# A two-layer hybrid diffusion trunk on one core: the channel mixer written as seven block products, in two phases, with the output feature-major

## The chip, the cores and the metric

One core of a Trainium2 chip runs the whole program. The metric is device time in microseconds (us) of one execution. The kernel before took 2927.19 us (median of three runs, 2924.78 to 2929.57).

Five engines share the work: PE (TensorE) does the matmuls, DVE (VectorE), ACT (ScalarE) and POOL (GpSimd) do elementwise work, and SP issues the DMAs. PE accumulates in eight PSUM banks (the tile PS, 8 x 512 columns); everything else lies in SBUF or in DRAM.

## What is computed

1,024 sample tokens and 128 prompt tokens, T = 1152 columns in all, pass two layers of width 1024. Layer 0 mixes tokens by latent attention and retention, layer 1 by a chunked gated MLP (gMLP). Each layer ends with the part that the change rewrites, the SwiGLU channel mixer with d_ff = 2816 = 22 tiles of 128:

```python
def swiglu(h, w_gate, w_up, w_down):
    return (jax.nn.silu(h @ w_gate) * (h @ w_up)) @ w_down
...
        hp = modulate(rmsnorm(xp, norm_g[l, 1]), sh2p, sc2p)
        hs = modulate(rmsnorm(xs, norm_g[l, 1]), sh2s, sc2s)
        xp = xp + g2p * swiglu(hp, w_ffn_gate[l], w_ffn_up[l], w_ffn_down[l])
        xs = xs + g2s * swiglu(hs, w_ffn_gate[l], w_ffn_up[l], w_ffn_down[l])
    y_prompt = rmsnorm(xp, final_norm_g)
    y_sample = rmsnorm(xs, final_norm_g)
```

Prompt and sample columns have their own shift, scale and gate (from `c_ctx` and `c`, the "conditioning"), so a piece of columns that crosses column 1024 is evicted in two instructions.

## The kernel before

Activations lie feature-major: the residual x is four tiles XT of [128, 2, 1152], read as eight feature tiles `X(f)`. Every large product is done in float32 precision by splitting both operands into a high part (ACT cast to fp32r) and a low part (DVE or POOL subtraction), and taking three passes: high x high, high x low, low x high (`groupA`, `three`). The split normalised activations are Hh and Hl in the tiles hq.

Columns go in three chunks of 384 (`CHUNKS`). In the channel mixer (`ffn`), a gate/up unit j takes two weight tiles and does, for each chunk, 8 x 3 matmuls for gate and 8 x 3 for up; ACT takes the silu out of PSUM, DVE multiplies, ACT and DVE split the result into one of three HID tiles in SBUF. After two units a down step `dn(j)` takes two rows of the down weight and does for each chunk and each of eight output tiles m 2 x 3 matmuls, and `resid` adds the bank onto x on DVE (`SCALAR_TENSOR_TENSOR x<-PS,mod,x`). So gate/up and down alternate, and the inner activations never leave SBUF.

Weights come through `Stream`: three staging slots ST of 512 KB, filled by SP, are split (`prep`) into a ring of five tiles RING (w). Background work (norms, squares, final output) stands in the queues `bg` and `bg2`; `fill` and `tick` issue it between products where the estimate of `Clocks` says that it won't hold up PE. PSUM banks rotate (`nxt`), so an eviction has several products' time.

`xnorm` normalises one chunk of 384 for the next block; the sum of squares over features is a matmul by ones. At the end `y_trans` turns x back by PE transposes (identity matmuls of 128 columns), `y_out` scales and SP stores token-major rows to o_ys and o_yp.

All instructions are recorded by one helper, so every row of the trace reads L126 (after the change L129); go by tiles and shapes.

Of the kernel before, what the change touches and what calls it, by code (L numbers as in the profile page):

```python
# [13 lines left out]
P = 128  # L14
# [3 lines left out]
CHUNKS = [(0, 384), (384, 384), (768, 384)]  # L18
NF = 22
# [20 lines left out]
class Clocks:  # L40
    """An estimate of when each engine is free and each piece of memory ready, to choose what to issue next."""
# [73 lines left out]
class Timed:  # L115
    """An engine whose instructions are also entered in the clocks."""
# [13 lines left out]
def body(nc, tc, ap):  # L130
# [45 lines left out]
    rgd = dp.tile([4, P, T], F32, name="rgd")  # L176

# [9 lines left out]
    sm = sb.tile([P, 5, 8], F32, name="sm")  # L187
    make_identity(nc, ident)
# [9 lines left out]
    att = [False]  # L198

    def nxt():  # L200
        if att[0]:
            return PS[:, 7]
        b = bank_i[0]
        bank_i[0] = step_bank(b)
        return PS[:, b]
# [9 lines left out]
    class Stream:  # L215
# [11 lines left out]
        def pump(self, force=False):  # L227
            moved = True
            while moved:
# [18 lines left out]
                if self.pi < self.di and self.pi not in self.stops:  # L248
                    it = self.items[self.pi]
                    now = clk.t["T"] + 1.0  # L250
                    if it["kind"] == "w":
# [37 lines left out]

        def take(self):  # L290
# [34 lines left out]
    def fill(aps=()):  # L325
        """Issues background work that does not hold up the tensor engine's next product, which reads aps."""
# [29 lines left out]
    def ada_raw(l, b, k, half):  # L356
        def fn(v):
            if k == 0 and half == 0 and ada_f:
                drain(ada_f.pop())
            for j in (2 * half, 2 * half + 1):  # L360
                o = (j % 2) * 512
                mm(ada_bank[32 * j:32 * j + 32], S32[:, k], v[:, o:o + 512], k == 0, k == 7)
            if k == 7 and half == 1:
                ada_f.append(ada_fin(l, b))
                bg.appendleft(ada_f[-1])
        src = ap["w_ada"][l, k * P:(k + 1) * P, 2048 * b + 1024 * half:2048 * b + 1024 * half + 1024]
        W.add(src, [1024], "raw", fn)
# [60 lines left out]
    def squares(ci, srcs, first=True, eng=V):  # L428
        acc = nt(ci % 2)
        for i, s in enumerate(srcs):  # L430
            n = s.shape[-1]
            if first and i == 0:
                S.activation(acc[:, :n], s, AF.Square)
            else:
                sqi[0] ^= 1
                q = nt(5 + sqi[0], n)
                S.activation(q, s, AF.Square)
                eng.tensor_tensor(acc[:, :n], acc[:, :n], q, ALU.add)
            yield

# [19 lines left out]
    def norm(ci, srcs, dh, dl, cnt, c0, n, A, B, f32out=None):  # L460
        yield [nt(ci % 2, n)]
        scale_cols(ci, cnt, n)
        yield [nt(2, n)]
        scale_bc(n)
        yield
        r = nt(2, n)
        m = len(srcs)
        ts = [nt(3 + i % 4, n) for i in range(m)]
        sg = [(cond, slice(s0 - c0, s0 - c0 + ln)) for cond, s0, ln in segs(c0, n)]

        def first(i):
            if i % 4 == 3:
                G.tensor_tensor(ts[i], srcs[i], r, ALU.mult)
                return
            for cond, s in sg:
                V.scalar_tensor_tensor(ts[i][:, s], srcs[i][:, s], A(i, cond), r[:, s], ALU.mult, ALU.mult)

        def high(i):
            if i % 4 == 3:
                for cond, s in sg:  # L480
                    S.activation(ts[i][:, s], ts[i][:, s], AF.Identity, scale=A(i, cond), bias=B(i, cond))
            if B is None or i % 4 == 3:
                S.copy(R(dh[i]), ts[i])
# [1488 lines left out]
```

## Time and profile before

| | us |
|---|---|
| median of three runs | 2927.19 |
| lowest, highest | 2924.78, 2929.57 |
| span of the profiled execution, first to last instruction | 2919.6 |
| median less that span | 7.6 |
| PE busy | 2846.6 (97%) |
| DVE, ACT, POOL busy | 1309.1 (45%), 849.6 (29%), 311.9 (11%) |
| mean granted TensorE clock | 0.989 |

The page gives no other time for the profiled execution than its span, so sums are made against the span, and the 7.6 us are added at the end. The channel mixers are the stretches from about 860 to 1740 us (layer 0) and from about 2090 to 2910 us (layer 1). Matmuls overlap in the pipeline of PE, so the mean ns of one is longer than the distance from one start to the next; the price of a matmul in a dense run is that distance.

### The profile page before, as it was taken

What the parts mean: (1) busy time and instruction counts of PE and PEld (TensorE: products, weight loads), DVE (VectorE), ACT (ScalarE), POOL (GpSimd) and SP (SyncE); (2) the same over time, 40 slices, a digit from 0 to 9 for tenths busy, and PEclk for the clock granted to TensorE, in tenths of its full rate; (3) what the DMA queues carried; (4) which work ended last, traced back from release to release, by engine and by line L of the source; (5) the groups of instructions that cost most, each with busy time, mean ns of one, the idle gap of its engine ahead of it and who ended that gap; (6) DMA issues with size and microseconds to landing.
All of it is one profiled execution on the core that took longest, in us unless ns stands there. A gap on an engine that the chain in (4) does not pass through costs nothing. (4 is left out here: it accounts for less than half of the span.)

```text
span 2919.6 us, 40063 instructions
## 1 busy us (share of the span) xinstructions
PE 2846.6 (97%) x16583; PEld 2698.9 (92%) x16583; DVE 1309.1 (45%) x2478; ACT 849.6 (29%) x1575; POOL 311.9 (11%) x235
## 2 busy tenths in 40 slices
PE   6999998999999999999999999999999999999999
PEld 5986897888989899999999987999999999999999
DVE  5651235888463333333443354354533334333433
ACT  5552224776251111111111143232411111111115
POOL 1120013665110000000000031000100000000001
PEclk8999998999999999999999999999999999999999
DMA  8395426322322212222211131141111111111111
GB/s 293 88 276 173 136 78 187 83 78 79 116 73 87 77 61 87 87 75 85 66 37 36 44 109 36 33 127 30 45 43 44 44 44 43 36 38 44 44 30 65
DMA packets 223467, 237.62 MB, mean 81 GB/s; under 512 B 15595, under 2 KB 193526, under 8 KB 221750
## 3 DMA queue, kind: packets, MB, share of 16 engines
q1 hardware_dynamic: 220880, 232.23, 26.3%
q8 instruction: 130, 2.13, 0.3%
q10 hardware_dynamic: 2406, 2.85, 0.3%
q14 instruction: 51, 0.42, 0.0%
HBM read 193.37 MB, written 41.66 MB: 81 GB/s over the span
## 5 line engine op out<-in xcount | busy, mean ns | idle before, releaser
L126 PE MATMUL PS<-hq,w 128*128 128x384 f32 x9216 | 1650.7, 338 | 12.3 <-ACT hq L126 7.4
L126 PEld LDWEIGHTS PS<-hq,w 128*128 128x128 f32 x9216 | 1615.1, 188 | 48.3 <-ACT SC L126 14.7
L126 PE MATMUL PS<-h,w 128*128 128x384 f32 (+1 forms) x3182 | 563.4, 337 | 3.5 <-DVE x L126 3.5
L126 PEld LDWEIGHTS PS<-h,w 128*128 128x128 f32 (+1 forms) x3182 | 554.2, 188 | 11.3 <-DVE x L126 10.0
L126 DVE SCALAR_TENSOR_TENSOR x<-PS,mod,x 128x384 f32<-128x384 f32 (+2 forms) x768 | 371.3, 513 | 228.1 <-PE PS L126 227.6
L126 DVE TENSOR_TENSOR w<-ST,w 128x1024 fp32r<-128x1024 f32 (+1 forms) x201 | 232.2, 1165 | 496.8 <-ACT w L126 496.5
L126 ACT ACTIVATE SC<-PS 128x384 f32<-128x384 f32 (+1 forms) x162 | 80.3, 496 | 895.4 <-PE PS L126 889.4
L126 DVE TENSOR_TENSOR SC<-PS,SC 128x384 f32<-128x384 f32 (+2 forms) x139 | 77.5, 558 | 458.3 <-PE PS L126 454.7
L126 ACT CAST w<-ST 128x1024 fp32r<-128x1024 f32 (+1 forms) x201 | 194.6, 980 | 102.4 <-PE PS L126 80.0
L126 ACT CAST h<-SC 128x384 fp32r<-128x384 f32 (+2 forms) x141 | 72.1, 511 | 495.4 <-DVE SC L126 493.3
L126 POOL TENSOR_TENSOR SC<-SC 128x384 f32<-128x384 f32 x35 | 35.6, 1017 | 1602.8 <-ACT SC L126 1600.5
L126 PE MATMUL PS<-w,hq 128*128 128x512 f32 x648 | 158.6, 402 | 1.4 <-POOL hq L126 1.3
L126 PEld LDWEIGHTS PS<-w,hq 128*128 128x128 f32 x648 | 122.0, 191 | 39.7 <-issue 10.3
L126 DVE TENSOR_TENSOR h<-SC,h 128x384 fp32r<-128x384 f32 (+2 forms) x141 | 79.4, 563 | 83.7 <-ACT h L126 83.5
L126 PE MATMUL PS<-w,w 96*128 96x512 f32 x384 | 108.5, 418 | 3.9 <-ACT w L126 2.4
L126 DVE TENSOR_REDUCE sm<-PS 128x1 f32<-128x1152 f32 (+1 forms) x72 | 89.0, 1236 | 22.1 <-PE PS L126 21.3
L126 DVE TENSOR_TENSOR x<-PS,x 128x512 fp32r<-128x512 f32 (+2 forms) x161 | 94.5, 623 | 0.8
L126 PEld LDWEIGHTS PS<-w,w 96*128 96x128 f32 x384 | 69.1, 194 | 17.0 <-issue 3.0
L126 PE MATMUL PS<-x,hq 128*128 128x256 f32 x504 | 77.4, 296 | 5.1 <-DVE sm L126 5.1
L126 ACT CAST x<-PS 128x512 fp32r<-128x512 f32 (+2 forms) x161 | 79.4, 546 | 6.4 <-PE PS L126 4.9
L126 PEld LDWEIGHTS PS<-x,hq 128*128 128x128 f32 x504 | 68.4, 194 | 9.5 <-DVE sm L126 6.2
L126 POOL TENSOR_TENSOR SC<-x,SC 128x384 f32<-128x384 f32 x24 | 28.8, 1200 | 446.1 <-ACT SC L126 395.8
(163 smaller groups left out, 1831.7 us busy)
## 6 DMA issues: line engine op xcount, KB each, us to landing
ST<-in_w_ada SPq DMA_DIRECT2D x80, 512.0 KB, 3.9
ST<-in_w_ffn_gate SPq DMA_DIRECT2D x44, 512.0 KB, 3.9
ST<-in_w_ffn_up SPq DMA_DIRECT2D x44, 512.0 KB, 4.9
ST<-in_w_ffn_down SPq DMA_DIRECT2D x44, 512.0 KB, 3.6
ST<-in_w_in_ab SPq DMA_DIRECT2D x19, 512.0 KB, 4.9
xtd<-x SPq DMA_DIRECT2D x24, 384.0 KB, 6.3
x<-xtd SPq DMA_DIRECT2D x24, 384.0 KB, 4.5
hq<-in_w_ada SPq DMA_DIRECT2D x8, 1024.0 KB, 11.8
```

Of the source, the lines that this page charges most:

```text
L126: return fn(*args, **kw)
```

## The change

**Column pieces.** The chunks of the two output projections and of gMLP's u become four pieces of 288 (`NAT`, or `PAIRED`: 0, 2, 1, 3). x is laid out anew as `xh(c, q)`: c is the first or second 288 of each half of 576 columns, q the half of the features. Piece (c, h) holds columns 576h + 288c to 576h + 288c + 287.

**Seven products.** The mixer's products are taken as 2 x 2 blocks by the Winograd form of Strassen's method: seven block products in the place of eight, with sums of blocks ahead of and behind them. The right operand's blocks are the halves of the features by the halves of the columns; `rnorm` writes the seven right blocks (RIGHT) from the normalised x, in the hq, h and x tiles; x itself is spilled to DRAM (`pspill`) before and loaded again (`preload`) for the down phase. The left operand is two weight tiles (gate and up, or two 128-column pieces of down); `Mixer.prep` makes the seven left blocks with four additions and seven splits (ACT cast, DVE subtraction), additions on DVE in gate/up and on POOL in down.

**Two phases.** First all 22 gate/up units, each 7 x 4 x 3 x 2 = 168 matmuls of 288; POOL combines every second pair of inner activations (`combine`) into the right blocks of the down phase, which SP writes to DRAM (hcd). Then down: six groups of d_ff tiles (2 tiles, then five times 4) by four pairs of output tiles m; `hload` brings the blocks back from hcd, `hsplit` splits them (ACT copy, POOL subtraction of 576 columns). Each of a step's seven products is added onto its x block on DVE (`down.add`); three of the products accumulate on top of an earlier one in the same pair of banks, so they wait for that one's eviction.

**The rest.** The conditioning products of layer 1 take two weight halves together (`ada_pair`); the reciprocal roots for the norm are made on 96 partitions (`rstd`); gMLP's tiles go in the order `ORDER`; the output is one feature-major array o_y, so the PE transposes at the end go, and the host turns it.

```diff
-    def ffn(l, done, last):
...
+        BANKS = (0, 1, 0, 2, 0, 2, 0)
+        OPENS = (0, 1, 3)
...
+            def split(i, src):
...
+                S.copy(R(z[0]), src)
+                V.tensor_tensor(R(z[1]), src, z[0], ALU.subtract)
...
+            def put(o, a, b, op):
+                add.tensor_tensor(o, a, b, op)
+            (a11, a12), (a21, a22) = A
+            yield from split(0, a11)
+            yield from split(1, a12)
+            yield from split(6, a22)
+            put(a22, a21, a22, ALU.add)
+            yield
+            put(a21, a11, a21, ALU.subtract)
+            put(a11, a22, a11, ALU.subtract)
+            yield from split(2, a11)
...
+        def product(self, i, key, nk, right, cs, pair):
+            s = self.left[key][i][0][0]
+            for c in cs:
+                b = PS[:, 2 * pair + c, :HN]
+                fill([s[:, :, 0:P], right(i, 0, c)])
+                n = 0
+                for k in range(nk):
+                    z = right(i, k, c)
+                    for a, h in ((0, 0), (0, 1), (1, 0)):
+                        TE.matmul(b, lhsT=R(s[:, a, P * k:P * k + P]), rhs=R(z[:, h]), start=n == 0 and i in self.OPENS,
+                                  stop=n == 3 * nk - 1, skip_group_check=True)
+                        n += 1
...
+        def steps(self, key, nk, right, cs, evict, keep=False, before=None, after=None):
+            pairs = [(self.turn + b) % 3 for b in self.BANKS]
+            for i in range(7):
+                if before:
+                    before(i)
+                self.product(i, key, nk, right, cs, pairs[i])
+                next(self.gen, None)
...
+                evict(i, PS[:, 2 * pairs[i] + cs[0]:2 * pairs[i] + cs[-1] + 1, :HN])
...
+        def hsplit(self):
+            _, g, op, c = self.todo.popleft()
+            d = self.right[g, op, c][0]
+            S.copy(R(d[:, 0]), d[:, 1])
+            G.tensor_tensor(R(d[:, 1]), d[:, 1], d[:, 0], ALU.subtract)
...
+            def add(f, h, b):
+                for n, c in enumerate(cs):
+                    x = xp(f, c, h)
+                    for cond, s in psegs(c, h):
+                        V.scalar_tensor_tensor(x[:, s], b[:, n, s], mcol(l, 5, f, cond), x[:, s], ALU.mult, ALU.add)
+            to = ((m, 0), (m, 0), (m, 1), (m + 4, 1), (m + 4, 1), (m, 1), (m + 4, 0))
...
+                if u < NF - 1:
+                    self.gen = self.prep(u + 1, 4, V)
+                else:
+                    self.narrow()
+                    self.gen = self.prep((0, 0), 1, G)
```

In the order of the instructions the whole program has 13,392 matmuls of 288 columns and 1,152 of 384 of these kinds where it had 12,384 of 384. Three places are shown.

PE in the down step of layer 0, before (h are HID tiles, w ring tiles; a name in brackets is the engine whose count the instruction waits for):

```order
L126 MATMUL PS<-h_86_6776,w_98_7675 128x384 x3
L126 MATMUL PS<-h_88_6778,w_97_7619 128x384 [waits DVE_49]
L126 MATMUL PS<-h_88_6778,w_97_7619 128x384 x2
L126 MATMUL PS<-h_86_6776,w_98_7675 128x384 x3
L126 MATMUL PS<-h_88_6778,w_97_7619 128x384 [waits DVE_49]
```

and PE in the down phase of layer 0 now (hq and h hold right blocks, w left blocks):

```order
L129 MATMUL PS<-hq_14_226,w_85_6674 128x288 [waits DVE_49,Activation_49]
L129 MATMUL PS<-hq_14_226,w_85_6674 128x288 x5
L129 MATMUL PS<-hq_20_535,w_85_6674 128x288 [waits DVE_49]
L129 MATMUL PS<-hq_20_535,w_85_6674 128x288 x5
L129 MATMUL PS<-hq_14_226,w_87_7000 128x288 [waits DVE_49,Activation_49]
L129 MATMUL PS<-hq_14_226,w_87_7000 128x288 x5
L129 MATMUL PS<-h_82_6671,w_87_7000 128x288 [waits DVE_49]
L129 MATMUL PS<-h_82_6671,w_87_7000 128x288 x5
```

Each group of six matmuls now waits for DVE, and where a left block is new also for ACT; the blocks that it reads were made during the step before.

DVE in the down step, before (only pairs of evictions, for a step's third chunk):

```order
L126 SCALAR_TENSOR_TENSOR x_75_6033<-PS,mod_92,x_75_6033 128x256 [waits PE_49]
L126 SCALAR_TENSOR_TENSOR x_75_6033<-PS,mod_92,x_75_6033 128x128
L126 SCALAR_TENSOR_TENSOR x_76_6037<-PS,mod_92,x_76_6037 128x256 [waits PE_49]
L126 SCALAR_TENSOR_TENSOR x_76_6037<-PS,mod_92,x_76_6037 128x128
L126 SCALAR_TENSOR_TENSOR x_76_6037<-PS,mod_92,x_76_6037 128x256 [waits PE_49]
```

and DVE in the down phase now:

```order
L129 SCALAR_TENSOR_TENSOR x_93_11648<-PS,mod_93,x_93_11648 128x288 [waits PE_49]
L129 SCALAR_TENSOR_TENSOR x_95_11650<-PS,mod_93,x_95_11650 128x288 [waits PE_49]
L129 TENSOR_TENSOR w_85_6674<-ST,w_85_6674 128x256 [waits Activation_49]
L129 SCALAR_TENSOR_TENSOR x_93_11648<-PS,mod_93,x_93_11648 128x288 [waits DVE_49,PE_49]
L129 SCALAR_TENSOR_TENSOR x_95_11650<-PS,mod_93,x_95_11650 128x288 [waits DVE_49,PE_49]
L129 TENSOR_TENSOR w_85_6674<-ST,w_85_6674 128x256 [waits Activation_49]
L129 SCALAR_TENSOR_TENSOR x_93_11648<-PS,mod_93,x_93_11648 128x288 [waits PE_49]
L129 SCALAR_TENSOR_TENSOR x_95_11650<-PS,mod_93,x_95_11650 128x160 [waits PE_49]
L129 SCALAR_TENSOR_TENSOR x_95_11650<-PS,mod_93,x_95_11650 128x128
```

Between two evictions there stands now a subtraction for a left block of the next step, behind ACT's cast; it has both inputs in SBUF.

PE at the start of layer 0's mixer now, in unit 0's pass over the first pieces (c = 0):

```order
L129 MATMUL PS<-ones,SC 96x2 [waits DVE_49]
L129 MATMUL PS<-ones,SC 96x2 x2
L129 MATMUL PS<-h_83_6672,w_88_7006 128x288 [waits Activation_49]
L129 MATMUL PS<-h_83_6672,w_88_7006 128x288 x11
L129 MATMUL PS<-ST,S_92 32x512 [waits DMAHW7_49,DMAHW3_49]
L129 MATMUL PS<-ST,S_92 32x512
L129 MATMUL PS<-ST,S_92 32x512 [waits DMAHW4_49]
L129 MATMUL PS<-ST,S_92 32x512
L129 MATMUL PS<-h_84_6673,w_86_6922 128x288 [waits DVE_49]
L129 MATMUL PS<-h_84_6673,w_86_6922 128x288 x11
L129 MATMUL PS<-SC,ones 128x288 [waits DVE_49,Activation_49]
L129 MATMUL PS<-SC,ones 128x288 [waits Activation_49]
```

The sums of squares of the second pieces (`ones,SC 96x2`) and the spreading of their roots (`SC,ones 128x288`) stand inside that pass, so the right blocks of the second pieces can only be made behind them.

## Rows read from the trace of the kernel before

**Rows 1.** The page: busy time, granted clock and traffic over the whole span.
```profile
PE 2846.6 (97%) x16583; PEld 2698.9 (92%) x16583; DVE 1309.1 (45%) x2478; ACT 849.6 (29%) x1575; POOL 311.9 (11%) x235
...
PEclk8999998999999999999999999999999999999999
...
GB/s 293 88 276 173 136 78 187 83 78 79 116 73 87 77 61 87 87 75 85 66 37 36 44 109 36 33 127 30 45 43 44 44 44 43 36 38 44 44 30 65
```

**Rows 2.** Stretches: us; PE, PEld, DVE, ACT, POOL busy (x); PEclk, DMA share, GB/s.
```profile
460.00:755.00 295.00, 279.75 (x1854) 250.23 (x1854) 224.03 (x448) 200.17 (x412) 164.83 (x107) 0.96 0.35 95
...
860.00:1740.00 880.00, 874.23 (x4960) 838.04 (x4959) 349.96 (x608) 159.39 (x257) 28.46 (x23) 1.00 0.23 71
...
2090.00:2890.00 800.00, 800.00 (x4581) 800.00 (x4581) 309.93 (x529) 138.27 (x220) 11.43 (x12) 1.00 0.14 41
2890.00:2919.60 29.60, 23.04 (x168) 22.43 (x166) 12.88 (x28) 18.41 (x35) 5.85 (x6) 0.88 0.29 107
```

**Rows 3.** PE by form: out<-in xcount | busy us, mean ns | idle before.
```profile
L126 PE MATMUL PS<-hq,w 128*128 128x384 f32 x9216 | 1650.7, 338 | 12.3 <-ACT hq L126 7.4 <-ACT SC L126 2.2 <-POOL hq L126 1.3
...
L126 PE MATMUL PS<-x,hq 128*128 128x256 f32 x504 | 77.4, 296 | 5.1 <-DVE sm L126 5.1
```

**Rows 4.** PE timeline inside a gate/up unit: start us, us, what xcount.
```profile
1059.59 33.86 PE L126 MATMUL PS<-hq,w 128*128 128x384 f32 x192
1093.38 1.06 PE L126 MATMUL PS<-ST,S 128*32 128x512 f32 x8
```

**Rows 5.** PE timeline inside the attention, columns as before.
```profile
603.92 0.60 PE L126 MATMUL PS<-ident,h 128*128 128x128 f32 x4
604.36 0.93 PE L126 MATMUL PS<-ident,SC 128*128 128x128 f32 x7
...
606.52 0.87 PE L126 MATMUL PS<-x,hq 128*128 128x256 f32 x6
607.23 0.39 PE L126 MATMUL PS<-h,h 96*128 96x128 f32 x2
```

**Rows 6.** DVE timeline inside a down step of layer 1.
```profile
2391.09 0.74 DVE L126 SCALAR_TENSOR_TENSOR x<-PS,mod,x 128x256 f32<-128x256 f32 x2 [0.31 <-PE PS L126]
```

**Rows 7.** DVE by form, whole span.
```profile
L126 DVE SCALAR_TENSOR_TENSOR x<-PS,mod,x 128x384 f32<-128x384 f32 x384 | 229.4, 615 | 148.4 <-PE PS L126 147.9
...
L126 DVE SCALAR_TENSOR_TENSOR x<-PS,mod,x 128x256 f32<-128x256 f32 x192 | 92.7, 483 | 79.7 <-PE PS L126 79.7
...
L126 DVE SCALAR_TENSOR_TENSOR x<-PS,mod,x 128x128 f32<-128x128 f32 x192 | 65.6, 342 | 0.0
...
L126 DVE TENSOR_TENSOR SC<-SC 128x384 f32<-128x384 f32 x45 | 25.2, 560 | 17.4 <-ACT SC L126 15.5
...
L126 DVE TENSOR_TENSOR x<-x,h 128x128 f32<-128x128 f32 x48 | 10.4, 282 | 16.0 <-ACT x L126 16.0
```

**Rows 8.** DVE by form in the attention, 460 to 755 us.
```profile
L126 DVE TENSOR_TENSOR w<-ST,w 128x256 fp32r<-128x256 f32 x19 | 11.8, 646 | 8.2 <-ACT w L126 8.1
```

**Rows 9.** POOL by form, whole span.
```profile
L126 POOL TENSOR_TENSOR SC<-SC 128x384 f32<-128x384 f32 x35 | 35.6, 1017 | 1602.8 <-ACT SC L126 1600.5
...
L126 POOL TENSOR_TENSOR SC<-SC,x 128x512 f32<-128x512 f32 x8 | 10.2, 1270 | 55.3 <-ACT SC L126 53.9 <-DMA ST<-in_w_ada 1.4
```

**Rows 10.** POOL by form in the attention, 460 to 755 us.
```profile
L126 POOL TENSOR_TENSOR SC<-SC,sm 128x128 f32<-128x128 f32 x8 | 3.2, 400 | 12.8 <-DVE sm L126 12.8
```

**Rows 11.** DVE timeline at the first split of layer 0's mixer.
```profile
880.67 1.11 DVE L126 TENSOR_TENSOR h<-SC,h 128x384 fp32r<-128x384 f32 x1 [3.52 <-ACT h L126]
...
882.83 0.56 DVE L126 TENSOR_TENSOR h<-SC,h 128x384 fp32r<-128x384 f32 x1 [0.58 <-ACT h L126]
```

**Rows 12.** POOL timeline at the same place.
```profile
880.36 1.02 POOL L126 TENSOR_TENSOR hq<-SC,hq 128x384 fp32r<-128x384 f32 x1 [1.70 <-issue]
```

**Rows 13.** Timeline of the end, PE and SP's queue.
```profile
2908.07 1.28 PE L126 MATMUL PS<-h,w 128*128 128x384 f32 x6
...
2915.55 0.60 SPq L126 DMA_DIRECT2D o_yp<-ST  x1
```

More of the change, by code (lines that the diff above doesn't have):

```diff
@@ L287, in prep, with loaded, block, free @@
                     yield
+            self.st.append(it["st"])
+        def loaded(self, n):
+            return (self.pi + n <= self.di and self.pi not in self.stops
+                    and all(i["kind"] == "block" for i in self.items[self.pi:self.pi + n]))
+        def block(self):
+            while self.items[self.pi]["kind"] != "block" or self.pi >= self.di:
+                p = self.pi, self.di
+                self.pump(force=True)
+                assert (self.pi, self.di) != p
+            self.pi += 1
+            return self.items[self.pi - 1]
+        def free(self, it):
             self.st.append(it["st"])
@@ L441, in scale_cols, with psegs @@
+    def psegs(c, h):
+        c0 = piece(c, h)
+        return [(cond, slice(s0 - c0, s0 - c0 + ln)) for cond, s0, ln in segs(c0, HN)]
     def scale_cols(ci, cnt, n, d=2):
@@ L1740, in body, with last0, done0 @@
+    mixer = Mixer(0)
+    proj_out(0, done=(wo_rs, wo_b), ks=KS, mix=mixer)
+    yield "C"
+    def last0(c, m):
+        for f in (m, m + 4):
+            for h in range(2):
+                bg_add(squares(c, h, [f], f == 0, G))
+    def done0(c):
+        nr[c] = bg_add(xnorm(1, 0, c))
+    mixer.run(last0, done0)
     yield "D"
@@ L1916, in body, with last1, gen, done1 @@
-    ffn(1, done1, last1)
+    def last1(c, m):
+        def gen():
+            for f in (m, m + 4):
+                for h in range(2):
+                    yield from squares(c, h, [f], f == 0, V if c else G)
+                    x = xp(f, c, h)
+                    S.activation(x, x, AF.Copy, scale=P2[:, 19 + f:20 + f])
+                    yield
+        g = bg_add(gen())
+        if c:
+            drain(g)
+    def done1(c):
+        def gen():
+            yield from rstd(c)
+            for h in range(2):
+                r = acc2(c)[:, HN * h:HN * h + HN].unsqueeze(1).to_broadcast([P, 2, HN])
+                for i in range(4):
+                    x = xp2(i, c, h)
+                    (G if i == 3 else V).tensor_tensor(x, x, r, ALU.mult)
+                    o = piece(c, h)
+                    SY.dma_start(out=ap["o_y"][2 * i:2 * i + 2, :, o:o + HN].rearrange("f p t -> p f t"), in_=x)
+                    yield
+        g = bg_add(gen())
+        if c:
+            drain(g)
@@ L1917, in body @@
+    mixer.run(last1, done1)
     while bg:
```

763 lines of the change are left out of this document (488 added, 275 removed).

## The prediction

> **What bounds the kernel now.** [...] In both channel mixers (860 to 1740 and 2090 to 2890 us) PE is busy 99% and 100% at a clock of 1.00, while DVE has 350 of 880 us and POOL 28 [rows 2]. So the mixers are bounded by the number of matmul columns and nothing else: fewer columns are time won, up to the point where another engine takes over. DVE has slack in the old order, POOL lies almost idle.
>
> **The price of a matmul.** Lengths in the groups (338 ns for 384 columns [rows 3]) overlap, so I take distances between starts. 192 matmuls of 384 columns begin at 1059.59 and the next kind at 1093.38: 0.176 us each [rows 4]. In the attention 6 of 256 columns take 607.23 - 606.52, 0.118 each, and 4 of 128 take 604.36 - 603.92, 0.110 each [rows 5]. From 256 to 384 that is 0.453 ns a column, so 288 lies at 0.118 + 32 x 0.00045 = 0.1325 us. [...]
>
> **The sum, part by part (against the span of 2919.6).**
>
> *Products.* The order has 12,384 matmuls of 384 columns before, and now 13,392 of 288 and 1,152 of 384. 12,384 x 0.176 = 2179.6; 13,392 x 0.1325 + 1,152 x 0.176 = 1977.2. That is -202 us. 72 transposes of 128 columns at the end go, 72 x 0.110: -8. Together **-210**, if PE never waits more than before.
>
> *Start of each mixer.* The second pieces' right blocks are made behind the sums and root spreads that stand inside unit 0's first pass. That pass gives a cover of 84 x 0.1325 = 11.1 us. DVE needs for them some 12 evaluations of 288 columns at 0.52 (between 0.483 and 0.615 [rows 7]) and 18 differences or splits of 576 columns at 0.75 (0.560 for 384, 0.282 for 128 [rows 7], continued): about 20 us, and the chain of ACT, PE and DVE ahead of it takes some 4. So 13 a layer: **+26**.
>
> *Between the phases.* Eight loads of x of 0.59 MB, 4.7 MB, come at once; at 293 GB/s, the highest slice [rows 1], that is 16 us, and the first down blocks are queued behind them on SP. The cover is the last pass of gate/up, 11.1 us, and what is left of the one ahead. I take 8 a layer: **+16** (none to 30).
>
> *Down steps, groups 1 to 4 (16 a layer, 32 in all).* A step is 84 matmuls, 84 x 0.1325 = 11.13 us of PE. DVE has seven evictions in two column pieces each. A 256 and a 128 together take 0.74, 0.085 less than 483 + 342 apart [rows 6, 7], and 288 lies at 0.516 by the same line. Three evictions miss the prompt: 2 x 0.516 - 0.085 = 0.945. Four have a piece split at column 1024: 1.06. That is 7.08 us. Then come seven subtractions of 256 columns for the next step's left blocks, 0.42 undisturbed (between 282 and 560 [rows 7]): 2.9. Sum 10.0, under PE's 11.13.
>
> But the subtractions have two inputs in SBUF, and POOL is busy now: four additions of 256 columns (0.70, between 400 and 1017 [rows 9, 10]) and 3.5 splits of 576 (1.40, from 1017 and 1270 for 384 and 512 [rows 9]), 7.7 us, 69% of a step. What that does to DVE the trace shows: a subtraction of 384 columns that begins while POOL runs takes 1.11 us and its like 0.56 when POOL is still; the long one ends when POOL's 880.36 + 1.02 is over [rows 11, 12]. [...]
>
> For the mean I take the nearest row: in the attention POOL is busy 165 of 295 us, 56% [rows 2], and 19 subtractions of just this form take 0.646 [rows 8], 0.226 above 0.42. At 69% that is 0.28 each, 2.0 a step. The step is then 7.08 + 7 x 0.70 = 12.0 us of DVE against 11.13: **+28** over 32 steps. Bounds: no wait (0), and half a POOL split for each, 0.70 (+123). Each group of six matmuls now waits for an eviction, and the eviction stands behind a subtraction that may wait for POOL: this is the wait that the change adds, and PE is what is queued behind it.
>
> *Group 0* has half the products a step (42, 5.57 us) and the same evictions: 7.08 and seven subtractions of 128 columns at 0.28 and some lock time, 10.0. Eight steps x 4.4: **+35**. *Group 5* goes by one piece at a time: 5.57 of PE against 3.6 + 3.9 of DVE in the six steps that still prepare a next one: **+12**.
>
> *Gate/up in steady state.* A unit is 168 x 0.1325 = 22.3 us. DVE has some 9.5 (four PSUM operations of 576 columns at about 0.75, seven splits and four additions of 512 at 0.6), POOL 4.2, ACT about 8. A bank's eviction has a whole product, 3.2 us. Nothing ends last there but PE: **+6** for stray waits (none to 40, if the combined activations' stores hold up POOL's buffers). Spills and stores of about 9.4 MB a layer lie beside 480 us of matmuls; with 71 GB/s in that stretch now [rows 2] they cost nothing. Without that cover they would take some 32 us a layer at 293 GB/s.
>
> *The end.* Before, the last product group ends near 2908.1 and the span at 2919.6, 11.5 us later [rows 13]. Now the last piece's norm, scaling and 1.2 MB of stores follow the last step: about 16. **+9** with the first piece's output in the way.
>
> Sum: -210 + 26 + 16 + 28 + 35 + 12 + 6 + 9 = -78. 2919.6 - 78 + 7.6 (the median lies so far above the span) = **2849 us**. A difference under 0.2%, 5.9 us, can't be told from none.
>
> **The rivals.**
>
> *DVE keeps pace.* DVE and POOL fall into step, so that POOL works while DVE evicts from PSUM, which the lock doesn't touch. Then groups 1 to 4 cost nothing, group 0 loses 15 and group 5 loses 6: 2849 - 28 - 20 - 6 = **2795**. For it: most of DVE's work in a step is evictions. Against: 10.0 of 11.13 us leaves little room.
>
> *The lock takes the gain (slower).* Place: the down phase, where 322 subtractions (224 in groups 1 to 4, 56 in group 0, 42 in group 5) stand between evictions that PE waits for. Each 0.1 us of mean wait above 0.28 costs 32 us. At 0.52 the gain of 78 is gone; at 0.70, half a POOL split each time, the kernel takes 2849 + 322 x 0.42 = **2984**. For it: the single wait of 0.55 [rows 11]. Against: with POOL at 56% the mean over 19 was 0.226 [rows 2, 8], though POOL's instructions there are longer. PE waiting also drags the clock: where it was busy 95%, 0.96 was granted [rows 2], which on 500 us of down phase is 20 more.
>
> *SP's queue.* Stores of combined activations wait for POOL, and weight loads stand behind them in the same queue. If a unit in two loses 2 us, 44 units lose 44: **2895**. Against: three staging slots are loaded ahead.
>
> *Loads in series.* If a weight load of its own stood ahead of each matmul, the 2,160 matmuls more would be paid in full. [...] The starts in rows 4 and 5 speak against it: 384 columns take 0.176, and loads are recorded beside matmuls for all of the 800 us of the second mixer [rows 2]. [...]
>
> That the change doesn't do what it says is excluded by the order: the counts are there.
>
> **How the numbers follow.** Forecast 0.50 (own range 2810 to 2885), DVE keeps pace 0.28, the lock 0.12, SP's queue 0.06, loads in series or the upper price 0.04. The first, second and fourth are faster: 0.84. The lock gives 0.03 within 0.2% and 0.09 slower, the last 0.04 slower: 0.13. The range reaches down past the second case, to 2770, and up to 2920, a mean wait of 0.50; outside lie the loads in series, most of the lock and a tail at the bottom, 0.2.
>
> **What would show it.** Right: matmuls of 288 start 0.13 us apart in gate/up, PE there over 98% busy; in down's groups 1 to 4 steps of about 12 us, PE some 93% busy, waiting for DVE, and subtractions `w<-ST,w` of 256 columns near 0.7 us; group 0's steps near 10. Steps of 11.2 would show the second case, steps over 13.7 the lock. The prediction falls if gate/up itself runs above 23.5 us a unit, or if PE's idle time gathers at the mixers' starts, or if it waits for DMA.

## The result and the profile after

| | us |
|---|---|
| before, median of 4 runs beside it | 2925.99 |
| after, median of 4 runs (lowest, highest) | 3038.19 (3036.41, 3038.66) |
| after / before | 1.0384, 95% interval 1.0369 to 1.0398 |
| span before, after | 2919.6, 3034.6 |

The change made the kernel 3.8% slower: 112 us, where 78 less were forecast. The page of the changed kernel, for [rows 1]:

```profile
PE 2725.3 (90%) x18667; PEld 2562.6 (84%) x18667; DVE 1728.6 (57%) x3368; ACT 1132.8 (37%) x2335; POOL 903.7 (30%) x748
...
PEclk8999999999969999999899889999699999989998
...
GB/s 282 105 269 164 157 90 142 64 111 110 76 54 115 143 121 134 115 135 199 147 117 128 72 91 35 55 114 57 26 103 81 110 94 88 102 215 97 128 75 63
```

PE is busy 121 us less than before and idle 236 us more (3034.6 - 2725.3 against 2919.6 - 2846.6). No other engine is full. So the products did become cheaper, and all of it and more went into waits of PE. A PE timeline inside a gate/up unit of layer 1, for [rows 4]:

```profile
2335.92 8.13 PE L129 MATMUL PS<-hq,w 128*128 128x288 f32 x60
2343.89 1.75 PE L129 MATMUL PS<-x,w 128*128 128x288 f32 x12
```

60 matmuls of 288 columns take 2343.89 - 2335.92, 0.133 us each: the price in the sum was right. Where the waits lie is seen in stretches of layer 1 (unit 0; units 1 to 20; eight steps' length of down, from within the first step of group 2 to within the first of group 4), for [rows 2]:

```profile
2131.80:2202.00 70.20, 39.22 (x185) 34.87 (x186) 47.38 (x83) 38.65 (x81) 16.63 (x14) 0.63 0.10 31
2202.00:2648.50 446.50, 446.50 (x3361) 445.69 (x3361) 242.01 (x300) 140.16 (x242) 94.74 (x61) 1.00 0.30 95
2780.10:2887.00 106.90, 93.64 (x675) 90.92 (x673) 83.06 (x204) 35.68 (x88) 66.25 (x61) 0.98 0.39 121
```

Steady gate/up is as forecast: 20 units in 446.5 us, 22.3 each, PE never idle. Unit 0 takes 70.2 us for the same work, and the eight steps' length of down is 106.9 us, 13.4 a step, where 11.13 is PE's own and 12.0 was forecast. DVE is busy for 83 of these 106.9 us: it is not full.

Matmuls of 288 columns can be counted off (168 a unit, 42 or 84 a down step), so the start of each stage gives its length. Us of each, from the starts of its first matmul and the next stage's:

| stage | before | after |
|---|---|---|
| up to the first output projection | 732.9 | 725.9 |
| first output projection | 117.4 | 138.0 |
| mixer of layer 0 | 877.8 | 932.2 |
| gMLP, v | 120.9 | 114.6 |
| gMLP u and output projection | 214.2 | 221.2 |
| mixer of layer 1 | 845.8 | 884.3 |
| end | 10.6 | 18.5 |

And inside the mixers, beside the length that the products alone have:

| part | products alone | layer 0 | layer 1 |
|---|---|---|---|
| unit 0 (two passes) | 22.3 | 25.7 + 35.4 | 37.0 + 33.2 |
| units 1 to 20 | 445.2 | 488.4 (with the conditioning's matmuls) | 446.6 |
| unit 21 | 22.3 | 25.3 | 22.3 |
| down, group 0 | 22.3 | 48.6 | 48.3 |
| groups 1 to 4 | 178.1 | 214.0 | 213.9 |
| group 5, first pieces | 22.3 | 44.2 | 42.5 |
| group 5, second pieces | 22.3 | 50.5 | 40.6 |

In groups 1 to 4, steps m = 0 and 1 take 14.3 to 15.7 us, steps m = 2 and 3 11.9 to 13.0.

**What PE waits for in a down step.** All engines ahead of the fifth product of a step (m = 1 of group 3, layer 1; products one and two begin at 2841.54, three and four at 2844.72):

```profile
2841.54 3.34 PE L129 MATMUL PS<-h,w 128*128 128x288 f32 x24
2844.72 3.33 PE L129 MATMUL PS<-hq,w 128*128 128x288 f32 x24
...
2846.23 0.74 POOL L129 TENSOR_TENSOR ST<-ST 128x256 f32<-128x256 f32 x1
...
2847.01 0.41 ACT L129 CAST w<-ST 128x256 fp32r<-128x256 f32 x1 [7.29 <-POOL ST L129]
...
2847.45 0.43 DVE L129 TENSOR_TENSOR w<-ST,w 128x256 fp32r<-128x256 f32 x1 [3.33 <-ACT w L129]
2847.79 0.94 DVE L129 SCALAR_TENSOR_TENSOR x<-PS,mod,x 128x288 f32<-128x288 f32 x2
...
2848.64 1.11 DVE L129 TENSOR_TENSOR w<-ST,w 128x256 fp32r<-128x256 f32 x1
...
2849.67 1.05 DVE L129 SCALAR_TENSOR_TENSOR x<-PS,mod,x 128x288 f32<-128x288 f32 x3
...
2850.32 0.37 PE L129 MATMUL PS<-hq,w 128*128 128x288 f32 x1 [2.27 <-DVE x L129]
```

PE waits 2.27 us for an eviction on DVE. By `BANKS` and `OPENS` four of the seven products, not three, accumulate on an earlier one; the fifth does so on the third and needs its eviction, which begins at 2849.67. DVE itself stood still for 3.33 us, up to 2847.45: at the head of its queue was a subtraction for the next step's left block, waiting for ACT's cast, which waited for POOL's additions. Behind it stood the eviction of the second product, whose matmuls were done some 2.9 us before it began at 2847.79. DVE's groups in the same 106.9 us:

```profile
L129 DVE SCALAR_TENSOR_TENSOR x<-PS,mod,x 128x288 f32<-128x288 f32 x82 | 40.3, 508 | 1.8 <-PE PS L129 1.1
L129 DVE TENSOR_TENSOR w<-ST,w 128x256 fp32r<-128x256 f32 x58 | 32.9, 591 | 24.9 <-ACT w L129 24.9
```

24.9 us of idle time stand ahead of these subtractions, in nine waits that ACT's cast ended. (The first wait began before the stretch. DVE's idle time within it is 106.9 - 83.06, 3.0 us a step.) The lock is there too, that is, a DVE subtraction with both inputs in SBUF takes longer beside POOL: 591 ns against 417 undisturbed (in e16 below), 0.17 each on average (0.28 was forecast). It is uneven: 0.69 us in steps m = 0 and 1, where POOL has most of its splits, 0.48 in m = 2 and 3 (group 3, layer 1). Of the subtractions that lie whole in these 106.9 us, the 20 that began while POOL ran took 0.885 us on average, the 36 others 0.417. The evictions of 288 columns, which read PSUM, took the same beside POOL: 0.506 us for the 41 that began while it ran, 0.511 for the 41 others.

### The profile page after: what moved, and what is told of

It is laid out like the page before. It is cut to its first block, busy times and chain, and to the rows that moved or that the text cites. A ratio compares the mean times of both kernels' runs of the same rounds, so it can differ in the third digit from the quotient of the medians.

```text
span 3034.6 us, 48110 instructions
## 1 busy us (share of the span) xinstructions
PE 2725.3 (90%) x18667; PEld 2562.6 (84%) x18667; DVE 1728.6 (57%) x3368; ACT 1132.8 (37%) x2335; POOL 903.7 (30%) x748
## 4 chain that ended last, share of the span: by engine, by line
PE 52%; DVE 10%; POOL 8%; issue 7%; DMA 4%; ACT 3%; SPq 0%; DVEq 0%; POOLq 0%; ACTq 0%
PE PS L129 52%; DVE x L129 4%; POOL ST L129 4%; POOL hq L129 3%; DVE w L129 3%; DMA ST<-in_w_ffn_up 2%; ACT x L129 1%; ACT w L129 1%; DVE ST L129 1%; POOL h L129 1%; DVE SC L129 1%; DVE hq L129 1%; DMA w<-krd 1%; POOL SC L129 1%; ACT SC L129 0%
## 5 line engine op out<-in xcount | busy, mean ns | idle before, releaser
L129 PE MATMUL PS<-hq,w 128*128 128x288 f32 (+1 forms) x10200 | 1525.7, 308 | 169.1 <-DVE x L129 123.3
L129 PEld LDWEIGHTS PS<-hq,w 128*128 128x128 f32 x10200 | 1458.4, 194 | 221.8 <-issue 76.6
L129 DVE TENSOR_TENSOR w<-ST,w 128x512 fp32r<-128x512 f32 (+3 forms) x689 | 495.5, 739 | 567.9 <-ACT w L129 566.8
L129 ACT CAST w<-ST 128x512 fp32r<-128x512 f32 (+3 forms) x689 | 343.0, 535 | 667.6 <-POOL ST L129 374.1
L129 DVE SCALAR_TENSOR_TENSOR x<-PS,mod,x 128x288 f32<-128x288 f32 (+2 forms) x944 | 376.1, 442 | 127.8 <-PE PS L129 119.6
L129 PE MATMUL PS<-h,w 128*128 128x288 f32 (+1 forms) x2486 | 380.3, 302 | 38.8 <-DVE x L129 21.6
L129 PEld LDWEIGHTS PS<-h,w 128*128 128x128 f32 (+1 forms) x2486 | 348.2, 192 | 54.0 <-DVE SC L129 15.6
L129 PE MATMUL PS<-x,w 128*128 128x288 f32 (+1 forms) x1728 | 265.2, 302 | 22.7 <-ACT x L129 21.2
L129 PEld LDWEIGHTS PS<-x,w 128*128 128x128 f32 x1728 | 246.1, 191 | 26.0 <-ACT x L129 21.9
L129 POOL TENSOR_TENSOR hq<-hq 128x576 fp32r<-128x576 f32 x116 | 170.9, 1493 | 37.8 <-ACT hq L129 35.4
L129 PEld LDWEIGHTS PS<-w,hq 128*128 128x128 f32 x648 | 120.8, 188 | 33.2 <-issue 6.3
L129 DVE TENSOR_REDUCE sm<-PS 128x1 f32<-128x1152 f32 (+1 forms) x72 | 89.1, 1237 | 25.6 <-PE PS L129 24.9
```

Of the source, the lines that this page charges most:

```text
L129: return fn(*args, **kw)
```

## The experiments

Theory: a chain across the engines' queues (POOL addition, ACT cast, DVE subtraction) stands ahead of the evictions that PE waits for. Rivals: the lock between DVE and POOL; DVE's sum of work. Medians are compared with 3038 of the changed kernel; the kernel before, run beside each experiment, had medians from 2922 to 2928, so that distances of under some 5 us between experiments are not told apart. Step lengths are read as in the tables above, those of single steps in groups 2 to 4.

**e1_adds_dve.** Both `self.prep(..., G)` of the down phase:

```diff
-                        self.gen = self.prep(nxt_, GROUPS[nxt_[0]][1], G)
+                        self.gen = self.prep(nxt_, GROUPS[nxt_[0]][1], V)
```

> In the down phase the four additions for the left blocks go from POOL to DVE; nothing else moves. Theory (a chain across queues: in DVE's queue a subtraction waits for ACT's cast, which waits for POOL's additions, and the evictions that PE waits for stand behind it): the steps of groups 1 to 4 fall from 11.9 and 14.3 to 15.7 us to about 12 each, group 0 and the first half of group 5 lose some 2 us a step; together about 65 us less than the changed kernel, near 2975. Rival 1 (the SBUF lock between DVE and POOL): only what POOL's additions did to DVE goes, 10 us at most. Rival 2 (DVE's sum of work): four additions of 0.42 more a step, 40 to 55 us slower.

Measured 3028.03 (ratio to before 1.036, 1.0343 to 1.0377): 10 us less. Steps m = 2, 3 went to 11.7, but m = 0, 1 stayed at 14.4 to 16.0. All three expectations missed part of it, though the total alone is what the lock's rival allowed. The idle time ahead of the left blocks' subtractions did go, from 24.9 us to 4.3 in eight steps, but in steps m = 0 and 1 DVE is now full, 27.2 of 28.9 us. DVE's groups in eight steps, and its stretch for m = 0 and 1 of group 3 in layer 1:

```profile
L129 DVE TENSOR_TENSOR w<-ST,w 128x256 fp32r<-128x256 f32 x56 | 30.1, 560 | 4.3 <-ACT w L129 4.3
L129 DVE TENSOR_TENSOR ST<-ST 128x256 f32<-128x256 f32 x32 | 18.2, 570 | 0.5
```

```profile
2819.32:2848.17 28.85, 23.24 (x170) 22.39 (x169) 27.18 (x58) 10.45 (x24) 16.43 (x12) 1.00 0.38 120
```

DVE and POOL in such a step of this kernel:

```profile
2889.37 0.43 DVE L129 TENSOR_TENSOR ST<-ST 128x256 f32<-128x256 f32 x1
...
2892.59 6.10 POOL L129 TENSOR_TENSOR hq<-hq 128x576 fp32r<-128x576 f32 x4 [5.00 <-ACT hq L129]
...
2894.24 1.61 DVE L129 TENSOR_TENSOR ST<-ST 128x256 f32<-128x256 f32 x1
```

An addition of 0.43 takes 1.61 while POOL runs splits back to back: with the chain through POOL gone, the lock takes its place, since DVE now has four more instructions with two SBUF inputs. It costs most in the steps in which POOL runs splits without a pause: the additions take 0.72 us there on average and 0.42 in the others.

**e2_yields.**

```diff
             put(a11, a22, a11, ALU.subtract)
+            if add is G and nf < 4:
+                yield
+                yield
             yield from split(2, a11)
```

> The down phase's preparation of left blocks is the same work on the same engines, but the first subtraction that needs POOL's additions is put into DVE's queue two products later. Theory (chain across queues): steps with no splits of right blocks among POOL's additions fall from 11.9 to about 11.3 us, the others from 14.3 to 15.7 to about 12.5; some 50 us less than the changed kernel, near 2990. Rival 1 (SBUF lock) and rival 2 (DVE's sum of work): no work is gone, so under 10 us either way.

Measured 2963.24 (1.0136, 1.0115 to 1.0156): 75 us less, with the same work on the same engines. The steps of groups 2 to 4 are now 11.1, 12.9, 12.0, 11.1 (group 1 still has two of 13.5 to 16.2), group 0 went from 48 to 42 us, group 5's first half from 43 to 36. The eight steps of groups 3 and 4 of layer 1 in this kernel, columns as above, and DVE's subtractions there:

```profile
2768.40:2815.60 47.20, 45.28 (x339) 44.67 (x338) 42.07 (x101) 17.25 (x42) 33.07 (x30) 1.00 0.43 133
2815.60:2862.80 47.20, 45.35 (x339) 44.74 (x338) 42.07 (x101) 15.63 (x39) 33.05 (x30) 1.00 0.44 133
```

```profile
L129 DVE TENSOR_TENSOR w<-ST,w 128x256 fp32r<-128x256 f32 x56 | 31.6, 588 | 3.0 <-ACT w L129 2.8
```

DVE has the same 42 us in four steps, now in 47.2 us and not in 53.5. Its subtractions take 588 ns as before (591), so the lock is unchanged; what is gone is the idle time ahead of them. That is the theory: the order in the queue cost the time. Neither rival allows it.

**e3_no_hsplit** (a single run).

```diff
-            G.tensor_tensor(R(d[:, 1]), d[:, 1], d[:, 0], ALU.subtract)
+            S.copy(R(d[:, 1]), d[:, 1])
```

> Leaves out the subtraction that makes the low part of the down phase's right blocks (ACT copies in its place), so POOL has only its additions in the down steps. Theory (chain): POOL's additions are no longer queued behind subtractions of 1.4 us, so the steps of 14.3 to 15.7 us become 11.9 like their neighbours; the steps at 11.9 stay. Some 45 us less. Rival 1 (lock): all steps gain alike, 0.17 us times seven, some 1 us a step and 40 us in all, those at 11.9 too. Rival 2 (DVE's sum of work): no change over 10 us.

Measured 2972.25, 66 less. Steps m = 0, 1 fell to 12.1, steps m = 2, 3 stayed at 11.9, as the theory said. But this doesn't tell chain from lock: POOL's splits stand almost all in m = 0 and 1 (12 of 15 in e1's group 3), so their lock does too. DVE's subtractions in steps m = 0 and 1 of group 3, layer 1, first in the changed kernel, then here:

```profile
L129 DVE TENSOR_TENSOR w<-ST,w 128x256 fp32r<-128x256 f32 x14 | 9.3, 686 | 6.7 <-ACT w L129 6.7
```

```profile
L129 DVE TENSOR_TENSOR w<-ST,w 128x256 fp32r<-128x256 f32 x14 | 6.0, 449 | 4.9 <-ACT w L129 4.7
```

The two steps lost 4.4 us; the subtractions themselves became 3.3 shorter and the idle time ahead of them 1.8. In these steps the splits cost through the lock at least as much as through the chain; it is e2_yields that shows the chain alone.

**e4_begin_dve.** `self.prep(0, 4, G)` becomes `self.prep(0, 4, V)` in `begin`.

> The additions for the first gate/up unit's left blocks go from POOL to DVE. Theory for the mixers' starts: PE's wait of 9.7 us in the first pass of layer 1 is the same chain (POOL's four additions of 1.3 us, then ACT's cast, then what stands behind it), so it falls to some 4 us, and layer 0 likewise: 8 to 15 us less in all. Rival (the norm's own work on DVE sets the start): the wait moves to the next right block and the time stays within 5 us.

Measured 3029.45 (1.0366, 1.0346 to 1.0387): 9 less, with an interval that overlaps that of the changed kernel (1.0369 to 1.0398). Of the 9 only 3 lie in unit 0 of layer 0 (25.7 + 35.4, now 20.0 + 38.2); layer 1's took 36.9 + 33.2 as before. There the wait of 9.73 us fell to 4.39, as the theory said, and waits of 2.90 and 3.31 came behind it: the chain was there, but the rival's case decides.

**e5_evict_first.** With e2's edit; in `steps`:

```diff
-                next(self.gen, None)
-                if not keep:
-                    self.put(self.left[key][i][0])
                 evict(i, PS[:, 2 * pairs[i] + cs[0]:2 * pairs[i] + cs[-1] + 1, :HN])
+                next(self.gen, None)
+                if not keep:
+                    self.put(self.left[key][i][0])
```

> The two later products of e2_yields, and each product's eviction is put into the queues ahead of the preparation work of that place, not behind it; in gate/up too. Theory (evictions stand behind subtractions that wait): group 0 and the first half of group 5, where the cover is half, lose another 1 to 2 us a step, groups 1 to 4 little: 10 to 25 us below e2_yields' 2963. Rival (after e2_yields what is left is the lock and DVE's sum of work): within 5 us of it.

Measured 2953.34 (1.01, 1.0075 to 1.0125), 10 below e2, at the edge of what the theory said, and not at its place: group 0 lost 1.7 and 0.9 us in the two layers and group 5's first half 0.1 and 1.4, where 1 to 2 us for each of 16 steps were expected.

**e6_spread.** With e2's edit; `if self.todo and i % 2 and ...` ahead of `hsplit`.

> The two later products of e2_yields, and the down phase's splits of right blocks are issued at every second product at most, not at each. Theory for what e2_yields leaves (runs of POOL subtractions of 1.4 us each hold DVE's subtractions by the lock, 1.2 instead of 0.42): the steps of 12.9 and 12.0 us in groups 1 to 4 fall to about 11.5, 10 to 20 us below 2963. Rival (POOL's sum of work delays its additions): no gain, or slower, since the splits come nearer to their due time.

Measured 2967.36 (1.0148, 1.0127 to 1.0169), 4 above e2, not told apart from it. Steps m = 1, 2 did fall to 11.7 and 11.1, but m = 0 rose from 11.1 to between 13.3 and 14.4. That is what the rival expects of splits that come due at the group's start.

**e7_norm_dve.** With e2's edit; in `rnorm` and `xnorm` every product, low part and scaling that was `G` is `V`.

> The two later products of e2_yields, and POOL's part of the norms (a quarter of the scalings and some of the low parts) goes to DVE. Theory (chains through POOL): the third step of layer 0's last pass, where DVE waits for ACT and ACT for POOL, falls from 28.9 to under 20 us, and each mixer's start loses 5 us: 15 to 25 us below 2963. Rival (DVE's sum of work bounds the starts): each start grows by the moved work, some 5 us for each of the two norms: 10 to 20 us above 2963.

Measured 2943.71 (1.0067, 1.0044 to 1.0091), 20 below e2: unit 0's second pass fell from 35.3 and 33.2 to 29.5 in both layers, and the first mixer began 7 us earlier. In layer 1 the first pass took back what the second gave (37.1 to 41.8), and layer 1's gain lies ahead of it, where PE no longer waits 9.8 us between projection and mixer. The third step of the last pass only went from 28.9 to 26.7, so that part of the expectation failed.

**e8_no_second** (a single run): the second pieces' `rnorm` isn't called, and `right` returns `RIGHT[i, 0]`.

> Leaves out the norm and the right blocks of the second column pieces (c = 1) in both mixers; the products read the first pieces' blocks in their place. All else is the changed kernel. Theory (that norm, with its sums, roots, scalings, differences and splits in series, sets the length of the mixers' starts): unit 0's second pass falls from 35 and 33 us to about 12, and the first by some 5: 50 us below the changed kernel's 3038, near 2988. Rival (weights and left blocks set the start): the second pass stays over 22 us.

Measured 2975.38, 63 less. The second passes fell from 35.4 and 33.2 to 15.6 and 11.2, the first ones from 25.7 and 37.0 to 16.5 and 29.2. PE in this kernel at the start of layer 1's mixer:

```profile
2097.42 3.22 PE L129 MATMUL PS<-hq,w 128*128 128x288 f32 x12 [9.84 <-DVE x L129]
2110.37 6.38 PE L129 MATMUL PS<-hq,w 128*128 128x288 f32 x36 [9.73 <-ACT SC L129]
2120.24 6.56 PE L129 MATMUL PS<-h,w 128*128 128x288 f32 x36 [3.50 <-ACT SC L129]
2126.64 6.54 PE L129 MATMUL PS<-hq,w 128*128 128x288 f32 x48
```

Unit 0 is 59 us shorter in the two layers together, of 87 that it had over its products: the norm of the second pieces is most of its cost. What is left are the wait ahead of the first product (an eviction behind the first pieces' norm in DVE's queue) and, in layer 1, the wait of 9.73, at the place of POOL's additions for unit 0 (see e4).

**e9_all**: the edits of e2, e4, e5 and e7.

> The four parts that theory and runs point to together: two later products (e2_yields), eviction first (e5_evict_first), the norms off POOL (e7_norm_dve), the first unit's additions on DVE (e4_begin_dve). If they work at separate places their gains add: 75 + 10 + 20 + 9 below the changed kernel, 2925, about level with the kernel before. If the two that act on the starts take the same wait, 2935.

Measured 2936.21 (1.0043, 1.0029 to 1.0057): the gains of e4 and e7 do overlap, for unit 0 takes 54.5 and 71.4 us here and 54.3 and 71.3 in e7.

**e10_all_ahead3, e11_ahead3**: `AHEAD = 3.0`, on e9 and on the changed kernel. **e12_look3**: 3 from the first output projection on, on e9. In these and in e13 the sums of squares of the second pieces come after unit 0's first pass and overwrite its product for columns 576 to 863, which shares SC with them, so these four kernels compute those columns wrongly; their instructions are the same ones.

> As e9_all, and background work is issued up to 3 us ahead of PE by the kernel's own estimate, not 7. Theory (what stands ahead of evictions in DVE's queue makes PE wait): the wait of some 12 us in layer 0's last pass, where a whole norm of 13.7 us stands ahead of four evictions, and that of 10 us at the end of the projections, shrink; 10 to 25 us below e9_all. Rival (DVE's sum of work bounds these places, the order in the queue doesn't matter): within 5 us of e9_all.

> The changed kernel with 3 us in the place of 7 for background work, nothing else. Theory: background work and evictions share DVE's queue at the starts and in the last passes, not in the middle of the mixers, so 10 to 30 us below 3038, all of it at those places, the steps of groups 1 to 4 as they were. Rival: within 5 us of 3038.

> As e9_all, with background work issued up to 3 us ahead in the place of 7 from the first output projection on; the attention keeps its order. Theory (background work stands ahead of evictions in DVE's queue): the third step of layer 0's last pass falls from 26 to about 15 us and the wait at the end of the projections shrinks; 8 to 15 us below e9_all's 2936. Rival (DVE's sum of work bounds these places): within 5 us.

Measured 2927.91 (1.0019, 1.0008 to 1.0029), 3020.09 (1.033, 1.0313 to 1.0348) and 2937.72 (1.0039, 1.0025 to 1.0053). In layer 0's last pass the third step did fall, from 26.3 to 14.4 in e10 and 15.9 in e12, but the fourth step and the v products behind it then took 12 us longer (134 for 122): there the rival holds, DVE's sum of work. The first mixer starts at 846.9 in e10 and not at 858.7. Of these 12 us, 7.5 lie in the first output projection; e12 has them too and loses them in unit 0 (62.1 for 54.5). What e10 has beyond e12 (1.0019 against 1.0039) comes from the attention, the one place where the two differ.

**e13_late_spill**: on e12, spills of the second pieces are held until their `rnorm` begins.

> As e12_look3, and the spills of the last pieces of x are put into SP's queue when their norm starts, not when they are evicted. Theory for what is left of the starts (three spills stand 13 to 20 us at the head of SP's queue, waiting for evictions, with the second unit's weight loads behind them; ACT's cast waits for those weights with evictions behind it): unit 0's first pass falls from 41 to some 32 us in layer 1 and from 27 to 23 in layer 0; 8 to 15 us below e12_look3. Rival (the norm of the second pieces, already known to be most of the start, takes the wait over): within 4 us.

Measured 2935.84 (1.0032, 1.0018 to 1.0045), 2 below e12; unit 0's passes as before. A miss: the loads behind the spills are not what the start waits for.

**e14_split_early.** On e9: `hid_out` splits a right block (ACT cast, DVE subtraction into the free half of XT[3]) and stores both parts to an hcd twice as large; `spread` issues one at every second product; `hload` reads both parts; `hsplit` is left for group 5.

```diff
+            if g < 5:
+                z = XT[3].rearrange("p a t -> p (a t)")[:, T:2 * T].rearrange("p (a c n) -> p a c n", a=2, c=2)
+                S.copy(R(z[:, 0]), v)
+                V.tensor_tensor(R(z[:, 1]), v, z[:, 0], ALU.subtract)
...
```

**e15_split_look**: the same with 3 us ahead up to the first mixer, 7 from there. **e16_store_later**: e15 with the stores of a block one product after its split.

> As e9_all, and the right blocks of down's groups 0 to 4 are split into high and low part already in gate/up (ACT cast and DVE subtraction, one block at every second product), stored as two parts and loaded ready to use; the down phase has splits for group 5 alone. Theory (in the down phase POOL's splits hold DVE by the lock and delay POOL's additions, while in gate/up POOL, DVE and ACT have room): groups 1 to 4 go at 11.1 us a step, group 0 below 10, gate/up stays at 22.3 us a unit: 30 to 40 us below e9_all's 2936, so below the kernel before. Rival (the moved work makes evictions wait in gate/up): units grow by 1 us or more, 40 of them, and the gain is gone.

> As e14_split_early, with background work issued up to 3 us ahead in the attention and the first output projection, 7 from the first mixer on. Theory: the first mixer starts 10 us earlier (847 in the place of 859) and nothing else moves: 10 us below e14_split_early. Rival: the wait moves into that mixer's start, same time.

> As e15_split_look, with the two stores of each split block put into SP's queue one product after the split, not with it. In layer 0, where the conditioning's weights share the three staging slots, every second unit of e15_split_look takes 30 us: the stores stand at the head of SP's queue, waiting for ACT and DVE, with the next unit's weight loads behind them, and ACT's cast waits for those weights. Theory: these units fall to 24 us like their neighbours, ten of them: 50 to 60 us below 2950, near 2895, and so below the kernel before (2927) by about 1%. Rival (the stored bytes themselves, or the one scratch tile, delay the loads): the units stay above 27 us, under 25 us gained.

e14: 2961.97 (1.0119, 1.0096 to 1.0141), 26 above e9 where 30 to 40 below were expected. Down did as the theory said: all steps of groups 1 to 3 take 11.1 to 11.2 us. Layer 1's gate/up kept its 22.3 us, but in layer 0 every second unit took 30 us. SP's queue and ACT in one of those units:

```profile
1168.39 8.93 SPq L129 DMA_DIRECT2D hcd<-x  x4
...
1177.42 1.16 SPq L129 DMA_DIRECT2D ST<-in_w_ffn_up  x1
...
1182.58 0.62 ACT L129 CAST w<-ST 128x512 fp32r<-128x512 f32 x1 [5.36 <-DMA ST<-in_w_ffn_up]
```

A load of the up weight is issued behind stores that wait, and ACT's cast waits for it. e15: 2950.00 (1.0075, 1.0048 to 1.0102), 12 less, as expected. e16: **2893.39** (ratio 0.9888, 0.9871 to 0.9904), 1.1% faster than the kernel before; layer 0's units fell to 24. Not all of that is the seven products': the two mixers are 9 and 14 us shorter than before, but 13 us lie ahead of the first projection, where background work now runs 3 us ahead, and the kernel before wasn't run with that. Its stretches of layer 1 (units 1 to 20; groups 2 and 3 of down) and DVE's groups in groups 2 and 3:

```profile
2113.60:2559.00 445.40, 445.40 (x3362) 445.40 (x3361) 261.25 (x363) 175.68 (x303) 83.28 (x59) 1.00 0.40 135
2664.00:2753.00 89.00, 89.00 (x673) 89.00 (x672) 76.65 (x200) 18.05 (x56) 23.63 (x32) 1.00 0.73 234
```

```profile
L129 DVE SCALAR_TENSOR_TENSOR x<-PS,mod,x 128x288 f32<-128x288 f32 x81 | 41.1, 515 | 5.1 <-PE PS L129 4.8
L129 DVE TENSOR_TENSOR w<-ST,w 128x256 fp32r<-128x256 f32 x56 | 22.0, 417 | 0.0
```

PE is busy all of both stretches. The subtractions wait for nothing and take 417 ns: in these groups chain and lock are both gone.

## Why the prediction was wrong

The products were priced rightly; what failed is the price of the waits. Three terms failed: the starts of the mixers and group 5, both mis-sized many times over, and groups 1 to 4, whose wait was priced by the wrong rule. The prediction's own sign of falling, idle time of PE at the mixers' starts, is what came. Point by point, by the terms of its sum (beside the products alone; the kernel before had 9 us over its products in the whole of layer 1's mixer, 845.8 against 4,752 x 0.176):

- *Products, -210*: right in price. 0.133 us for 288 columns, steady gate/up at 22.3 us. "Loads in series" is refuted by the same stretch: weight loads were recorded for 445.7 of the 446.5 us in which PE was never idle. Neither did the upper price come, 0.154 (77.4 us over 504 matmuls of 256 columns [rows 3]).
- *Gate/up, +6*: 1 in layer 1. DVE's work, estimated at 9.5 us a unit, was 12.1 (242.01 us over 20 units; its subtractions and additions of 512 columns took 0.805 and 0.968 us on average, not 0.6), still far under PE's 22.3. In layer 0 the 20 units are 43 over the products; the conditioning's matmuls, 8 a unit at 1.06 [rows 4], are 21 of it and were there before. The other 22 stand against the +6; 11 of them are waits of PE for DVE.
- *Between the phases +16 and group 0 +35*: 26 a layer in group 0 and 3 in layer 0's last unit, 55. Right in sum, by luck in part: DVE's work in group 0 is as forecast, 9.6 us a step (10.0), but the rest came from its waits for ACT's cast, 9.6 us (group 0 fell to 42 in e2), and not from loads. Layer 1's group 0, columns as above, and what DVE and PE waited for there:

```profile
2670.80:2719.10 48.30, 32.65 (x170) 29.55 (x169) 38.50 (x100) 13.25 (x41) 29.23 (x32) 0.83 0.48 157
```

```profile
L129 DVE TENSOR_TENSOR w<-ST,w 128x128 fp32r<-128x128 f32 x21 | 10.8, 539 | 7.5 <-ACT w L129 7.5
L129 DVE TENSOR_TENSOR w<-ST,w 128x256 fp32r<-128x256 f32 x7 | 2.9, 442 | 2.1 <-ACT w L129 2.1
```

```profile
L129 PE MATMUL PS<-hq,w 128*128 128x288 f32 x168 | 32.8, 359 | 15.7 <-DVE x L129 15.3 <-ACT w L129 0.3
```

- *Groups 1 to 4, +28*: measured +72. This is the step that failed in kind. The prediction named the wait ("the eviction stands behind a subtraction that may wait for POOL") but priced it as a sum of DVE's durations plus the lock: 12.0 a step. DVE's own work was 10.4 with the lock, less than PE's 11.13, so by that rule nothing was to be lost. What was missing is the time in which DVE stands still, 3.0 us a step, because its subtraction waits for ACT's cast of what POOL has still to add, with POOL's splits ahead of those additions. e2_yields shows it: the same work in another order is 75 us shorter, and 40 of the 72 here are gone. Most of the other 32 went when POOL's splits left the down phase (e14: 359 us for these steps, e9 386), so the lock that those splits cause has a part in them.
- *Start of each mixer, +26*: the term most mis-sized. Unit 0 costs 39 and 48 us over its products, and PE waits 23.8 and 9.9 us ahead of it: 120 in all, where the prediction had 26. PE's waits there in layer 1 of the changed kernel:

```profile
2131.80 3.22 PE L129 MATMUL PS<-hq,w 128*128 128x288 f32 x12 [9.85 <-DVE x L129]
2144.74 7.16 PE L129 MATMUL PS<-hq,w 128*128 128x288 f32 x36 [9.73 <-ACT SC L129]
...
2168.77 0.61 PE L129 MATMUL PS<-hq,w 128*128 128x288 f32 x1 [2.93 <-ACT hq L129]
...
2187.89 0.61 PE L129 MATMUL PS<-x,w 128*128 128x288 f32 x1 [9.34 <-ACT x L129]
```

  The sum had 20 us of DVE for the second pieces against 11 of cover. It left out the first pieces' norm, whose end stands ahead of the projection's last eviction, unit 0's left blocks on the same engines, and that each right block is a chain of ACT, DVE and POOL in turn. e8_no_second shows the second pieces' norm to be 59 of it. The clock adds to it: 0.63 granted in that stretch, PE busy 39.2 us, a few of them for sums and roots, with 22.3 us of products.
- *Group 5, +12*: measured 50 in layer 0 and 38 in layer 1, the second largest miss. The second half was put at nothing, but the squares, the next norm and the output's scaling run on DVE there, and half the products cover them. By e12 the norm's part is DVE's work, not only its order: what one step wins, the next stage loses.
- *The end, +9*: 8. Right.

"The lock takes the gain" ended on the right side (slower) for another reason: it had the place, but its mean wait was 0.17, below the forecast's 0.28, far from the 0.52 from which it decides. "DVE keeps pace" is what e16 makes true, with steps of 11.1. "SP's queue" wasn't the cause here (e13), but became one in e14.

Three slips in the prediction's working change little. By rows 11 and 12 the long subtraction ends 0.40 us after POOL's instruction (880.67 + 1.11 against 880.36 + 1.02), not with it. The second case takes 20 off group 0 where its sentence says 15, so its sum is 2800. And most of the 7.6 us between median and span is the distance between runs: one run of the changed kernel took 3036.4 us with a span of 3034.6.

Not settled: what of the starts is DVE's sum and what its chains. In e16 they still cost 37 and 50 us over unit 0's products; group 5 costs 40 and 30 there, group 0 19 and 16.

## What to carry to other kernels

Seven products for eight paid here only when what feeds them was ready. When work is moved beside an engine that others wait for, a sum of durations against the time available is not enough: follow each engine's queue in its order (here an eviction stood 2.9 us behind a subtraction that waited), and ask what stands at its head, what that waits for, and which urgent instruction is behind. An edit that only reorders the same work (e2_yields) was worth 75 us here, and with three more (e9) the kernel went from 3.8% to 0.4% slower. Moving splits to a stretch where the engines had room, a store one product later, and less background work ahead of the first mixer then made it 1.1% faster.

## What the runs showed of the hardware

Taking additions from POOL to DVE (e1) didn't shorten the steps in which POOL has other work (14.4 to 16.0 us, without that move 14.3 to 15.7): a DVE addition with two SBUF inputs took 1.61 us while POOL ran back to back, and 0.43 alone. After PE had waited 9.85 us at the start of layer 1's mixer, a clock of 0.50 was granted for the next 3.2 us, and twelve matmuls took 3.22 us (twelve took 1.75 at 2343.89, where 1.00 was granted):

```profile
2131.80:2135.00 3.20, 3.20 (x12) 2.87 (x12) 2.57 (x7) 2.48 (x7) 0.00 (x0) 0.50 0.26 92
```

And 234 GB/s of transfers beside a PE that was busy 89.0 of 89.0 us (e16) cost nothing that can be seen.
